# A recurrent layer's convolution and gate product: work moved from GpSimd and VectorE to ScalarE and VectorE, in a decoder step

## The chip, the cores and the metric

One core of a Trainium2 chip runs the whole program. The metric is the device time of one execution in microseconds; three executions of the kernel before were timed. A profile of one execution (not one of the timed ones) gives the start and the length of each instruction on five engines: TensorE (PE, with its weight loads as PEld), VectorE (DVE), ScalarE (ACT), GpSimd (POOL) and SyncE (SP), and of each DMA.

## What is computed

One inference step of two layers over 1032 columns: 1024 positions of one new sequence (the prompt) and one new token for each of 8 samples. Layer 0 mixes with a recurrent block, layer 1 with sliding-window attention; behind each stands a squared-ReLU MLP. The change lies in the recurrent block:

```python
def recurrent_block(x, h0, conv_prev, ...):
    gate, xr = jnp.split(x @ w_in, 2, axis=-1)
    xc, conv_new = causal_conv(xr, conv_prev, conv_w, conv_b)    # 4 taps; conv_new: last 3 rows of xr
    y, h_new = rg_lru(xc, h0, w_a, b_a, w_x, b_x, lam)
    return (y * jax.nn.gelu(gate)) @ w_out, h_new, conv_new

# rg_lru, elementwise but for the two block products and the scan
r = sigmoid(x @ w_a + b_a);  i = sigmoid(x @ w_x + b_x)          # 4 blocks of 256 channels
log_a = -8 * r * softplus(-lam);  a = exp(log_a)
u = sqrt(-expm1(2 * log_a)) * (i * x)
h_t = a_t * h_(t-1) + u_t
```

The prompt starts with zero state. Each sample starts with three old rows of the convolution (`conv_prev`) and its own h. The last three rows of the convolution's input and the last h are outputs, for the prompt and for each sample.

## The kernel before

All activations lie transposed: a tile holds 128 channels (partitions) by 1032 columns, eight tiles (m = 0 to 7) for the 1024 channels. The prompt stands in columns 0 to 1023, the samples in the last 8. Matmuls are made in three passes of fp32r halves: each operand is split into a high part (a cast, on ScalarE) and a low part (a subtraction, on VectorE). A projection works on three chunks of 344 columns, one PSUM bank each, out of a ring of six banks P P P S S T; so a projection takes P P P or S S T, and the next but one needs the banks emptied.

The recurrent layer is a list of stages, `LRU` (L55): `c1 c0 x4 g0 c2 c3 r0 c4 x5 g1 c5 r1 x7 x6 g2 r2 c7 o5 c6 o0 o1 o3 g3 r3 o6 o2 o4 o7`, behind a first stage that makes x0 to x3 together (L1146).

- **x** (`xr_stage`, `conv_evac`, L1122 to L1144): the projection of tile m, 72 matmuls. VectorE empties each bank with a product by the token's norm factor into `xr` (L1127, at high priority). GpSimd then makes the first tap of the convolution and its bias, chunk by chunk, into `xc` (L1128).
- **c** (`conv`, L1130): the three other taps on VectorE over the prompt's columns (L1133); the samples' and the prompt's last rows copied aside for output (L1134, L1135); the samples' three old taps, three VectorE operations on 8 columns (L1137); then the split of `xc` (cast L253 on ScalarE, low part L254 on VectorE).
- **g** (`gates`, L1152): for block kb, r and i of its two tiles: four projections of 18 matmuls from the split tiles 2kb and 2kb+1, each emptied by three sigmoids on ScalarE (L1161, at high priority).
- **r** (`recur`, L1164): for the block's two tiles, x is put together again from its halves by GpSimd (L1170) into the tile `ys[m]`; GpSimd makes i*x (L1171). ScalarE then writes Tanh into `ys[m]` (L1173), Exp over r (L1175), and squares (L1180), each followed by an update of `ys[m]` on VectorE (L1181); then the root (L1183). VectorE makes the product with i*x (L1186), the scan over the prompt (L1187), the samples' single step (L1188, L1189) and a copy of the last h (L1190).
- **o** (`gate_out`, L1194): the gate's projection, GeLU on ScalarE, product into `ys[m]` on VectorE (L1201), split for the output projection.

[...]

Weights arrive on SP's queue two tiles ahead, in two buffers, and are split by `split_unit` (cast L165 on ScalarE, low part L166 on VectorE; two of all units on GpSimd). The states leave by three DMAs on SP's queue behind r3 (L1211 to L1213).

A scheduler sets the order of each engine's instructions when the program is built, from its own estimates; operations marked high priority are put first where they can be. On the chip each engine takes its instructions in that fixed order and waits at each for semaphores of the others. Tiles come from pools (33 buffers of the kind `A`, 12 of `W`); a tile's first writer waits until the buffer's last user is done.

Of the kernel before, what the change touches and what calls it, by code (L numbers as in the profile page):

```python
# [10 lines left out]
F32 = mybir.dt.float32  # L11
F32R = mybir.dt.float32r
AF = mybir.ActivationFunctionType
ALU = mybir.AluOpType
PSUM = bass.MemoryType.PSUM

P = 128
D = 1024
M8 = D // P
SEQ = 1024  # L20
NS = 8
T = SEQ + NS
# [37 lines left out]
def trunk(ctx: ExitStack, tc: tile.TileContext, I, O):  # L60
    nc = tc.nc
    pe, act, dve, pool, sp = nc.tensor, nc.scalar, nc.vector, nc.gpsimd, nc.sync

    cp = ctx.enter_context(tc.tile_pool(name="cp", bufs=1))
# [24 lines left out]
    def nm(s):  # L89
        cnt[0] += 1  # L90
        return f"{s}{cnt[0]}"

    def A(s="a"):
        return ap.tile([P, T], F32, tag="A", name=nm(s))
# [4 lines left out]
    def S(s="s"):  # L99
        return small["pool"].tile([P, CH], F32, tag="S", name=nm(s))  # L100
# [24 lines left out]
    def cs(c):  # L125
        return slice(c * CH, (c + 1) * CH)
# [12 lines left out]
    def V(n, m=0):  # L139
        o, _ = VEC[n]  # L140
        return vec[:, o + m:o + m + 1]

    def VV(n):
        o, w = VEC[n]
        return vec[:, o:o + w]
# [30 lines left out]
    for o in [("x", m) for m in range(4)] + LRU:  # L176
        if o[0] == "g":
            units.append(("gate", o[1], I["w_gate"][o[1]], W))
        elif o[0] in "xo":
            m = o[1] + (8 if o[0] == "x" else 0)  # L180
# [71 lines left out]
    def split_act_dve(hi, lo, src, sl, eng=dve):  # L252
        act.copy(r_(hi[:, sl]), src)  # L253
        eng.tensor_tensor(r_(lo[:, sl]), src, hi[:, sl], ALU.subtract)  # L254
# [831 lines left out]
            ensure(3)  # L1086

    sp.dma_start(con, I["con"])
    cst = cp.tile([P, M8, 4, NS], F32, name="cst")
    sp.dma_start(cst[:, :, 0:3, :], I["conv_state"])  # L1090
    h0 = cp.tile([P, M8, NS], F32, name="h0")
    sp.dma_start(h0, I["h_state"])
    cvp = cp.tile([P, M8, 3], F32, name="cvp")
    hno = cp.tile([P, M8, 1 + NS], F32, name="hno")


    sp8 = cp.tile([P, M8], F32, name="sp8")
    nsp8 = cp.tile([P, M8], F32, name="nsp8")
# [19 lines left out]
    ys = {}  # L1118
# [3 lines left out]
    def conv_evac(m, c, o):  # L1122
        if c == 0:
            xrc[m] = (A("xr"), A("xc"))
        xr, xc = xrc[m]
        with tc.high_priority():
            dve.tensor_tensor(xr[:, cs(c)], o, rx[:, cs(c)], ALU.mult)  # L1127
        pool.tensor_scalar(xc[:, cs(c)], xr[:, cs(c)], V("cw3", m), V("cb", m), ALU.mult, ALU.add)  # L1128

    def conv(m):  # L1130
        xr, xc = xrc.pop(m)
        for d, w in ((1, "cw2"), (2, "cw1"), (3, "cw0")):
            dve.scalar_tensor_tensor(xc[:, d:SEQ], xr[:, 0:SEQ - d], V(w, m), xc[:, d:SEQ], ALU.mult, ALU.add)  # L1133
        dve.tensor_copy(cst[:, m, 3, :], xr[:, SEQ:T])  # L1134
        dve.tensor_copy(cvp[:, m, :], xr[:, SEQ - 3:SEQ])  # L1135
        for k, w in ((2, "cw2"), (1, "cw1"), (0, "cw0")):
            dve.scalar_tensor_tensor(xc[:, SEQ:T], cst[:, m, k, :], V(w, m), xc[:, SEQ:T], ALU.mult, ALU.add)  # L1137
        hi, lo = A("xch"), A("xcl")
        split_act_dve(hi, lo, xc, slice(0, T))
        xcs[m] = (hi, lo)  # L1140

    def xr_stage(m):
        for c, o in enumerate(proj(unit("in", 8 + m, 3), hs)):
            conv_evac(m, c, o)  # L1144

    def xr_first():  # L1146
        ws = [unit("in", 8 + m, 3 - m) for m in range(4)]
        proj_many(ws, hs, conv_evac)
# [15 lines left out]
    def recur(kb):  # L1164
        ms = (2 * kb, 2 * kb + 1)
        for m in ms:
            i = rr[m, 1]
            xh, xl = xcs.pop(m)
            ys[m] = (W if m in (2, 3, 5, 7) else A)("t")
            pool.tensor_tensor(ys[m], xh, xl, ALU.add)  # L1170
            pool.tensor_tensor(i, i, ys[m], ALU.mult)  # L1171
        for m in ms:
            act.activation(ys[m], rr[m, 0], AF.Tanh, scale=sp8[:, m:m + 1])  # L1173
        for m in ms:
            act.activation(rr[m, 0], rr[m, 0], AF.Exp, scale=nsp8[:, m:m + 1])  # L1175
        for m in ms:
            r, t = rr[m, 0], ys[m]
            for c in range(NCH):
                a2 = S("a2")
                act.activation(a2, r[:, cs(c)], AF.Square)  # L1180
                dve.scalar_tensor_tensor(t[:, cs(c)], a2, 1.0, t[:, cs(c)], ALU.add, ALU.mult)  # L1181
        for m in ms:
            act.activation(ys[m], ys[m], AF.Sqrt)  # L1183
        for m in ms:
            r, i, t = rr.pop((m, 0)), rr.pop((m, 1)), ys[m]
            dve.tensor_tensor(i, t, i, ALU.mult)  # L1186
            dve.tensor_tensor_scan(t[:, :SEQ], r[:, :SEQ], i[:, :SEQ], 0.0, ALU.mult, ALU.add)  # L1187
            dve.tensor_tensor(t[:, SEQ:T], r[:, SEQ:T], h0[:, m, :], ALU.mult)  # L1188
            dve.tensor_tensor(t[:, SEQ:T], t[:, SEQ:T], i[:, SEQ:T], ALU.add)  # L1189
            dve.tensor_copy(hno[:, m, :], t[:, SEQ - 1:T])  # L1190

    gos = {}

    def gate_out(m):  # L1194
# [9 lines left out]
        gos[m] = (hi, lo)  # L1204

    stages = {"x": xr_stage, "c": conv, "g": gates, "r": recur, "o": gate_out}
    xr_first()
    for what, i in LRU:
        stages[what](i)
        if (what, i) == ("r", 3):  # L1210
            sp.dma_start(O["conv"][:, :, 3:27].rearrange("p m (k n) -> p m k n", k=3), cst[:, :, 1:4, :])  # L1211
            sp.dma_start(O["conv"][:, :, 0:3], cvp)
            sp.dma_start(O["h"], hno)  # L1213
    gl = [gos[m] for m in range(M8)]
    pin_tables()
    spill, spill0, spill1 = [tc.dram_tile([M8, P, T], F32, name=f"spill{i}") for i in range(3)]
# [130 lines left out]
def _build(arrays):  # L1347
    import concourse.bacc as bacc

    nc = bacc.Bacc("TRN2", target_bir_lowering=False, num_devices=1)  # L1350
    I = {n: nc.dram_tensor(n, a.shape, mybir.dt.from_np(a.dtype), kind="ExternalInput").ap() for n, a in arrays.items()}
    O = {n: nc.dram_tensor("o_" + n, s, F32, kind="ExternalOutput").ap() for n, s in _OUT_SHAPES.items()}
    with tile.TileContext(nc) as tc:
        trunk(tc, I, O)
    return nc
# [23 lines left out]
```

## Time and profile before

| | |
|---|---|
| Timed executions, median of 3 | 2039.52 us (2037.89 to 2041.62) |
| Profiled execution, span from first to last instruction | 2037.0 us |
| First matmul of the first MLP (L529), behind the recurrent layer and its output projection | 348.58 us from the span's start |

No time of the profiled execution outside its span is recorded; its span lies 2.5 us below the timed median. A row of a timeline gives start, length, engine, line, operation and tiles, and in square brackets the idle time of the engine before it with what ended that idle time. A row of groups gives the number of instructions, their sum and mean (ns), and the idle time before them. A row of windows gives the stretch, busy time (and instructions) of PE, PEld, DVE, ACT and POOL, the clock granted to TensorE as a share of full speed, the DMA engines' busy share and GB/s. A row of waits gives who waited for whom, the sum, the number of times and the longest. Matmuls overlap: one of 344 columns is shown with 0.32 us, while the next starts some 0.16 after it.

### The profile page before, as it was taken

Reading aid. Unit: us, or ns where it says so; the run is one execution under the profiler, and the core shown is the slowest. Engines: PE = TensorE matmul, PEld = TensorE weight load, DVE = VectorE, ACT = ScalarE, POOL = GpSimd, SP = SyncE. Lnnn points to the kernel's source line nnn. Section 1 sums busy time; section 2 is a strip of 40 time slices with the busy share of each in tenths; the row PEclk is TensorE's granted clock in tenths of the full one; section 3 lists DMA queues with packets and bytes.
Section 4 is the critical chain, followed back from the end, with each engine's and each line's share of the span. In section 5 each row is a group of like instructions: output and inputs, shape, how many; then the busy total and the mean of one; then the engine's idle time right before and its main releaser. Section 6 shows DMA issues by size and latency. Waiting matters only on the chain.

```text
span 2037.0 us, 38615 instructions
## 1 busy us (share of the span) xinstructions
PE 2002.6 (98%) x15094; PEld 1957.6 (96%) x15094; DVE 1413.5 (69%) x2673; ACT 1051.6 (52%) x2090; POOL 352.1 (17%) x562
## 2 busy tenths in 40 slices
PE   8989999999999999999999999999999999999999
PEld 8989999999999999999988887999999999999999
DVE  8888547876666767766846777569766666777663
ACT  6475635544344645555457776555434435555450
POOL 2541100000001233221003434100000003323220
PEclk9989999999999999999999999999999999999999
DMA  5112142343436778867443435612443447887683
GB/s 175 52 32 55 53 167 84 106 161 135 156 131 207 232 207 218 235 163 184 128 109 84 106 98 180 230 62 82 173 156 131 162 167 235 216 225 220 164 201 105
DMA packets 121047, 304.87 MB, mean 150 GB/s; under 512 B 20888, under 2 KB 53152, under 8 KB 120864
## 3 DMA queue, kind: packets, MB, share of 16 engines
q1 hardware_dynamic: 64864, 135.41, 21.2%
q0 software_dynamic: 28352, 98.30, 18.9%
q10 hardware_dynamic: 27648, 68.70, 9.3%
q8 instruction: 118, 1.93, 0.4%
q14 instruction: 65, 0.53, 0.1%
HBM read 176.22 MB, written 113.44 MB: 142 GB/s over the span
## 4 chain that ended last, share of the span: by engine, by line
PE 74%; issue 10%; DMA 4%; POOL 3%; DVE 3%; ACT 2%; SPq 0%; POOLq 0%; ACTq 0%
PE bD L529 45%; PE bP L226 11%; PE bS L226 6%; PE bP L768 4%; PE bT L226 3%; DMA tl<-hsum 2%; PE bO L889 2%; PE bS L848 1%; PE bT L868 1%; POOL tl L542 1%; DMA spill<-ho 1%; POOL spill L652 1%; PE bN L714 1%; DMA spill<-he 1%; PE bS L796 1%
## 5 line engine op out<-in xcount | busy, mean ns | idle before, releaser
L529 PE MATMUL bD<-op,op 128*128 128x258 f32 x5376 | 648.5, 283 | 0.0
L529 PEld LDWEIGHTS bD<-op,op 128*128 128x128 f32 x5376 | 647.9, 189 | 0.3
L529 PE MATMUL bD<-tl,op 128*128 128x258 f32 x4704 | 571.6, 284 | 4.5 <-ACT ho L633 4.5
L529 PEld LDWEIGHTS bD<-tl,op 128*128 128x128 f32 x4704 | 570.0, 190 | 6.0 <-ACT ho L633 4.9
L542 POOL DMA_DIRECT2D tl<-hsum x196 | 115.1, 672 | 898.3 <-ACT op L395 422.0
L396 DVE TENSOR_TENSOR op<-ws,op 128x512 fp32r<-128x512 f32 (+2 forms) x288 | 168.5, 598 | 84.7 <-ACT op L395 84.6
L633 ACT COPY ho<-bD 128x516 f32<-128x516 f32 x144 | 85.0, 590 | 226.9 <-PE bD L529 226.9
L402 DVE TENSOR_TENSOR tl<-tl 128x516 fp32r<-128x516 f32 x196 | 130.6, 692 | 94.5 <-ACT tl L401 89.3
L395 ACT CAST op<-ws 128x512 fp32r<-128x512 f32 (+2 forms) x288 | 153.4, 550 | 41.4 <-DVE op L396 23.4
L633 ACT COPY he<-bD 128x516 f32<-128x516 f32 x144 | 83.9, 583 | 169.5 <-PE bD L529 169.5
L396 DVE TENSOR_TENSOR op<-raw,op 128x512 fp32r<-128x512 f32 (+2 forms) x216 | 124.0, 597 | 63.0 <-ACT op L395 63.0
L395 ACT CAST op<-raw 128x512 fp32r<-128x512 f32 (+2 forms) x216 | 114.1, 549 | 44.1 <-PE bD L529 20.3
L401 ACT CAST tl<-tl 128x516 fp32r<-128x516 f32 x196 | 115.3, 628 | 3.5 <-DMA tl<-hsum 3.5
L646 ACT ACTIVATE ho<-ho 128x1032 f32<-128x1032 f32 x32 | 34.2, 1069 | 107.3 <-DVE ho L645 107.3
L166 DVE TENSOR_TENSOR wl<-raw,wh 128x1024 fp32r<-128x1024 f32 (+1 forms) x57 | 68.1, 1201 | 25.0 <-ACT wh L165 20.1
L641 DVE TENSOR_TENSOR ho<-bD,ho 128x516 f32<-128x516 f32 x72 | 50.0, 694 | 43.5 <-PE bD L529 43.4
L859 POOL TENSOR_SCALAR se<-se,den 128x256 f32<-128x256 f32 (+1 forms) x128 | 66.0, 520 | 75.9 <-DVE den L857 73.9
L165 ACT CAST wh<-raw 128x1024 fp32r<-128x1024 f32 (+1 forms) x60 | 58.6, 988 | 35.3 <-DMA raw<-w_in 14.7
L652 POOL DMA_DIRECT2D spill<-ho x32 | 28.6, 894 | 259.8 <-DVE ho L641 249.1
L852 DVE CUSTOM_DVE_ANT_0 se<-bS,bias,nsink 128x256 f32<-128x256 f32 (+1 forms) x128 | 56.4, 461 | 21.7 <-PE bS L848 16.6
L855 ACT ACTIVATE se<-se,den 128x257 f32<-128x257 f32 (+1 forms) x128 | 63.0, 495 | 14.7 <-DVE den L852 13.1
L637 DVE TENSOR_TENSOR ho<-bD,ho 128x516 f32<-128x516 f32 x72 | 49.8, 691 | 20.5 <-PE bD L529 13.5
(299 smaller groups left out, 3741.9 us busy)
## 6 DMA issues: line engine op xcount, KB each, us to landing
tl<-hsum POOLq DMA_DIRECT2D x196, 258.0 KB, 7.1
raw<-w_up SPq DMA_DIRECT2D x64, 512.0 KB, 3.8
raw<-w_dn SPq DMA_DIRECT2D x64, 384.0 KB, 6.6
spill<-ho POOLq DMA_DIRECT2D x32, 516.0 KB, 5.7
spill<-he POOLq DMA_DIRECT2D x32, 516.0 KB, 7.1
hsum<-ho ACTq DMA_DIRECT2D x28, 516.0 KB, 3.6
hsum<-he ACTq DMA_DIRECT2D x28, 516.0 KB, 2.7
hsum<-ts ACTq DMA_DIRECT2D x28, 516.0 KB, 3.5
```

Of the source, the lines that this page charges most:

```text
L166: eng.tensor_tensor(r_(lo[:, sl]), raw[:, sl], hi[:, sl], ALU.subtract)
L226: pe.matmul(o, lhsT=r_(wt[:, col(k):col(k) + P]), rhs=r_(xt[:, cs(c)]), start=(k == first and a == 0), stop=(k == final and a == 2))
L395: act.copy(r_(t[:, 0:n]), src)
L396: dve.tensor_tensor(r_(t[:, n:2 * n]), src, t[:, 0:n], ALU.subtract)
L401: act.copy(r_(hi), lo)
L402: dve.tensor_tensor(r_(lo), lo, hi, ALU.subtract)
L529: pe.matmul(d[:, 512 * b:512 * b + QT], lhsT=r_(wt[:, j * P:j * P + P]), rhs=r_(xt[:, QT * b:QT * b + QT]), start=first and j == 0 and a = ...
L542: pool.dma_start(t[:, n:2 * n], src)
L633: last["copy"] = act.copy(t, f).ins
L768: pe.matmul(ps[c], lhsT=r_(wt[:, k * P:k * P + P]), rhs=r_(xt[:, cs(c)]), start=(k == 0 and a == 0), stop=(k == M8 - 1 and a == 2))
L855: act.activation(se[:, u, 256 - n:257], se[:, u, 256 - n:257], AF.Exp, scale=-1.0, bias=dn[:, u:u + 1], accum_out=dn[:, 2 + u:3 + u])
L859: pool.tensor_scalar(e, e, dn[:, 2 + u:3 + u], 0.0, ALU.mult, ALU.add)
```

## The change

Five edits in the recurrent layer:

1. The first tap with its bias leaves `conv_evac` and becomes, in `conv`, one ScalarE activation over all 1032 columns (scale and bias per partition).
2. The three old taps of all samples and tiles are summed once ahead of the layer, by five GpSimd operations, into `scs`; in `conv` one GpSimd addition on 8 columns takes their place.
3. x and i*x move from GpSimd to VectorE. For blocks 0 to 2, x gets a tile of its own, `x2`; block 3 keeps using `ys[m]`.
4. The samples' single step of h moves from VectorE to GpSimd.
5. The copies of states into collecting tiles and SP's three DMAs go. GpSimd's queue issues one DMA of the samples' old rows, one of 11 columns for each tile's last rows (from `xr`), and one of 9 columns for each tile's h (from `ys[m]`).

The host's code that puts the outputs together is fitted to the new layout.

```diff
@@ -1086,13 +1086,18 @@
             ensure(3)
 
     sp.dma_start(con, I["con"])
-    cst = cp.tile([P, M8, 4, NS], F32, name="cst")
-    sp.dma_start(cst[:, :, 0:3, :], I["conv_state"])
+    cst = cp.tile([P, M8, 3, NS], F32, name="cst")
+    sp.dma_start(cst, I["conv_state"])
     h0 = cp.tile([P, M8, NS], F32, name="h0")
     sp.dma_start(h0, I["h_state"])
-    cvp = cp.tile([P, M8, 3], F32, name="cvp")
-    hno = cp.tile([P, M8, 1 + NS], F32, name="hno")
-
+    pool.dma_start(O["conv"][:, :, 0:2 * NS].rearrange("p m (k n) -> p m k n", k=2), cst[:, :, 1:3, :])
+    scs = cp.tile([P, M8, NS], F32, name="scs")
+    scp = cp.tile([P, M8, NS], F32, name="scp")
+    for k in range(3):
+        w = VV(f"cw{k}").unsqueeze(2).broadcast_to([P, M8, NS])
+        pool.tensor_tensor(scp if k else scs, cst[:, :, k, :], w, ALU.mult)
+        if k:
+            pool.tensor_tensor(scs, scs, scp, ALU.add)
 
     sp8 = cp.tile([P, M8], F32, name="sp8")
     nsp8 = cp.tile([P, M8], F32, name="nsp8")
@@ -1125,16 +1130,14 @@
         xr, xc = xrc[m]
         with tc.high_priority():
             dve.tensor_tensor(xr[:, cs(c)], o, rx[:, cs(c)], ALU.mult)
-        pool.tensor_scalar(xc[:, cs(c)], xr[:, cs(c)], V("cw3", m), V("cb", m), ALU.mult, ALU.add)
 
     def conv(m):
         xr, xc = xrc.pop(m)
+        act.activation(xc, xr, AF.Identity, scale=V("cw3", m), bias=V("cb", m))
+        pool.dma_start(O["conv"][:, m, 2 * NS:], xr[:, SEQ - 3:T])
         for d, w in ((1, "cw2"), (2, "cw1"), (3, "cw0")):
             dve.scalar_tensor_tensor(xc[:, d:SEQ], xr[:, 0:SEQ - d], V(w, m), xc[:, d:SEQ], ALU.mult, ALU.add)
-        dve.tensor_copy(cst[:, m, 3, :], xr[:, SEQ:T])
-        dve.tensor_copy(cvp[:, m, :], xr[:, SEQ - 3:SEQ])
-        for k, w in ((2, "cw2"), (1, "cw1"), (0, "cw0")):
-            dve.scalar_tensor_tensor(xc[:, SEQ:T], cst[:, m, k, :], V(w, m), xc[:, SEQ:T], ALU.mult, ALU.add)
+        pool.tensor_tensor(xc[:, SEQ:T], xc[:, SEQ:T], scs[:, m, :], ALU.add)
         hi, lo = A("xch"), A("xcl")
         split_act_dve(hi, lo, xc, slice(0, T))
         xcs[m] = (hi, lo)
@@ -1166,9 +1169,12 @@
         for m in ms:
             i = rr[m, 1]
             xh, xl = xcs.pop(m)
+            x = A("x2") if kb < 3 else None
             ys[m] = (W if m in (2, 3, 5, 7) else A)("t")
-            pool.tensor_tensor(ys[m], xh, xl, ALU.add)
-            pool.tensor_tensor(i, i, ys[m], ALU.mult)
+            if x is None:
+                x = ys[m]
+            dve.tensor_tensor(x, xh, xl, ALU.add)
+            dve.tensor_tensor(i, i, x, ALU.mult)
         for m in ms:
             act.activation(ys[m], rr[m, 0], AF.Tanh, scale=sp8[:, m:m + 1])
         for m in ms:
@@ -1185,9 +1191,9 @@
             r, i, t = rr.pop((m, 0)), rr.pop((m, 1)), ys[m]
             dve.tensor_tensor(i, t, i, ALU.mult)
             dve.tensor_tensor_scan(t[:, :SEQ], r[:, :SEQ], i[:, :SEQ], 0.0, ALU.mult, ALU.add)
-            dve.tensor_tensor(t[:, SEQ:T], r[:, SEQ:T], h0[:, m, :], ALU.mult)
-            dve.tensor_tensor(t[:, SEQ:T], t[:, SEQ:T], i[:, SEQ:T], ALU.add)
-            dve.tensor_copy(hno[:, m, :], t[:, SEQ - 1:T])
+            pool.tensor_tensor(t[:, SEQ:T], r[:, SEQ:T], h0[:, m, :], ALU.mult)
+            pool.tensor_tensor(t[:, SEQ:T], t[:, SEQ:T], i[:, SEQ:T], ALU.add)
+            pool.dma_start(O["h"][:, m, :], t[:, SEQ - 1:T])
 
     gos = {}
 
@@ -1207,10 +1213,6 @@
     xr_first()
     for what, i in LRU:
         stages[what](i)
-        if (what, i) == ("r", 3):
-            sp.dma_start(O["conv"][:, :, 3:27].rearrange("p m (k n) -> p m k n", k=3), cst[:, :, 1:4, :])
-            sp.dma_start(O["conv"][:, :, 0:3], cvp)
-            sp.dma_start(O["h"], hno)
     gl = [gos[m] for m in range(M8)]
     pin_tables()
     spill, spill0, spill1 = [tc.dram_tile([M8, P, T], F32, name=f"spill{i}") for i in range(3)]
@@ -1369,8 +1371,8 @@
     hp = h[0].reshape(1, 1, D)
     hsm = h[1:].reshape(1, NS, D)
     cv = o["conv"].transpose(2, 1, 0).reshape(27, D)
-    cvp = cv[:3].reshape(1, 1, 3, D)
-    cvs = cv[3:].reshape(3, NS, D).transpose(1, 0, 2).reshape(1, NS, 3, D)
+    cvp = cv[2 * NS:2 * NS + 3].reshape(1, 1, 3, D)
+    cvs = np.concatenate([cv[:2 * NS], cv[2 * NS + 3:]]).reshape(3, NS, D).transpose(1, 0, 2).reshape(1, NS, 3, D)
     kp = o["k"].reshape(256, P).T.reshape(1, 1, P, 4, 64)
     vp = o["v"].reshape(1, 1, P, 4, 64)
     ks = o["ks"].reshape(2, P, NS, P).transpose(2, 3, 0, 1).reshape(1, NS, P, 4, 64)
```

In the built programs the matmuls are the same on TensorE, with a few of block 1's fourth projection and x7 in another order. On ScalarE, block 0's twelve sigmoids stand ahead of the first taps of c2 and c3. On VectorE, x5's evacuations stood ahead of r0's updates of `ys`; they now stand behind r0's scans and c4's taps and low part. From the output projection on, the order is the same on every engine.

## Prediction

> **What bounds the kernel now.** The page comes first: one engine is busy nearly all the time.
>
> ```profile
> span 2037.0 us, 38615 instructions
> ## 1 busy us (share of the span) xinstructions
> PE 2002.6 (98%) x15094; PEld 1957.6 (96%) x15094; DVE 1413.5 (69%) x2673; ACT 1051.6 (52%) x2090; POOL 352.1 (17%) x562
> ```
>
> TensorE is the bound, so the change is worth only the time in which it makes TensorE stop more or less. The built programs hold the same matmuls, and behind the recurrent layer all engines' instructions stand in the same order; the answer lies between 40 and 300 us. Next come the list of TensorE's waits there and its timeline.
>
> ```profile
> PE bP L226 <- ACT ri L1161: 6.1, 3, 5.0
> PE bS L226 <- DVE xr L1127: 3.9, 1, 3.9
> ...
> 94.70 0.63 PE L226 MATMUL bP<-xch,wh 128*128 128x344 f32 x3
> ...
> 97.52 0.48 PE L226 MATMUL bS<-xch,wh 128*128 128x344 f32 x2
> ...
> 105.50 1.53 PE L226 MATMUL bP<-xch,wh 128*128 128x344 f32 x3 [4.99 <-ACT ri L1161]
> ...
> 113.82 0.42 PE L226 MATMUL bP<-hh,wh 128*128 128x344 f32 x1 [0.57 <-ACT ri L1161]
> ...
> 139.74 0.32 PE L226 MATMUL bP<-xch,wl 128*128 128x344 f32 x1
> 143.94 1.08 PE L226 MATMUL bS<-xch,wh 128*128 128x344 f32 x2 [3.88 <-DVE xr L1127]
> ...
> 148.59 0.63 PE L226 MATMUL bP<-xch,wh 128*128 128x344 f32 x3
> ...
> 105.50:110.60 5.10, 5.10 (x18) 4.64 (x18) 5.10 (x10) 5.04 (x7) 0.00 (x0) 0.57 0.00 0
> ```
>
> The gates of block 1 are four projections of 18 matmuls. The first runs from 94.70 to 97.52, so 18 take 2.82 at full clock. The second would end at 100.34; the third starts at 105.50, 5.16 late: it waits for banks that ScalarE's sigmoids have not emptied. The last row (busy times, then granted clock) shows what a stop leaves behind: 18 matmuls in 5.10 at a clock of 0.57, 2.28 lost. At 113.82 another 0.57 goes. After 139.74 (+0.16 for the matmul) TensorE stands until 143.94, 4.04, for x6's evacuation on VectorE; the next 18 matmuls last to 148.59, 4.65 instead of 2.82, 1.83 lost. So **13.9** us of stops (5.16+2.28+0.57+4.04+1.83) can be removed; the floor is 13.9 below now.
>
> Why ScalarE was late is in its own timeline:
>
> ```profile
> 83.25 1.43 ACT L1161 ACTIVATE ri<-bP,vec 128x344 f32<-128x344 f32 x3 [1.41 <-PE bP L226]
> 84.55 2.97 ACT L253 CAST xch<-xc 128x1032 fp32r<-128x1032 f32 x3
> 94.25 1.16 ACT L1173 ACTIVATE t<-ri,sp 128x1032 f32<-128x1032 f32 x1 [6.73 <-POOL ri L1171]
> ...
> 97.81 1.28 ACT L1175 ACT_TABLE_LOAD   x1
> 99.11 2.21 ACT L1175 ACTIVATE ri<-ri,nsp 128x1032 f32<-128x1032 f32 x2
> 101.22 2.37 ACT L1180 ACTIVATE a<-ri 128x344 f32<-128x344 f32 x6
> ...
> 104.90 1.42 ACT L1161 ACTIVATE ri<-bP,vec 128x344 f32<-128x344 f32 x3
> ...
> 107.63 1.06 ACT L1183 ACTIVATE t<-t 128x1032 f32<-128x1032 f32 x1
> ```
>
> After block 0's sigmoids ScalarE waits 6.73 for GpSimd's i*x, because Tanh overwrites the tile that holds x; then Exp and squares stand ahead of block 1's first sigmoid (104.90). That wait goes with the change. What comes late next is a matter of the order in which the new program's instructions stand, and there the forecast turns.
>
> **The change, part by part.** GpSimd loses these groups; VectorE loses the small ones below them.
>
> ```profile
> L1128 POOL TENSOR_SCALAR xc<-xr,vec 128x344 f32<-128x344 f32 x24 | 27.0, 1131 | 43.7 <-DVE xr L1127 33.7 <-DVE sp L1113 4.5 <-DVE sp L1110 3.6
> L1171 POOL TENSOR_TENSOR ri<-ri,t 128x1032 f32<-128x1032 f32 x8 | 23.3, 2928 | 12.0 <-ACT ri L1161 11.8
> L1170 POOL TENSOR_TENSOR t<-xch,xcl 128x1032 f32<-128x1032 f32 x8 | 21.1, 2646 | 58.1 <-PE bT L226 40.9 <-issue 10.3 <-ACT ri L1161 4.4
> ...
> L1137 DVE SCALAR_TENSOR_TENSOR xc<-cst,vec,xc 128x8 f32<-128x8 f32 x24 | 9.6, 408 | 0.1
> ...
> L1188 DVE TENSOR_TENSOR t<-ri,h 128x8 f32<-128x8 f32 x8 | 5.5, 690 | 0.0
> ...
> L1173 ACT ACTIVATE t<-ri,sp 128x1032 f32<-128x1032 f32 x8 | 9.2, 1158 | 15.1 <-POOL ri L1171 15.1
> ...
> 54.38 0.51 DVE L1127 TENSOR_TENSOR xr<-bS,rt 128x344 f32<-128x344 f32 x1
> ...
> 63.44 1.22 DVE L254 TENSOR_TENSOR xcl<-xc,xch 128x1032 fp32r<-128x1032 f32 x1
> ...
> 68.47 1.27 DVE L1133 SCALAR_TENSOR_TENSOR xc<-xr,vec,xc 128x1022 f32<-128x1022 f32 x1
> ...
> 110.33 2.28 DVE L1187 TENSOR_TENSOR_SCAN t<-ri,ri 128x1024 f32<-128x1024 f32 x1
> 112.53 0.14 DVE L1188 TENSOR_TENSOR t<-ri,h 128x8 f32<-128x8 f32 x1
> ...
> 143.38 0.93 DVE L1127 TENSOR_TENSOR xr<-bS,rt 128x344 f32<-128x344 f32 x2
> ...
> 73.99 0.99 ACT L1161 ACTIVATE ri<-bS,vec 128x344 f32<-128x344 f32 x2 [4.57 <-PE bS L226]
> ```
>
> GpSimd gives up 71.4 us, none of it on the path beyond the stops above. VectorE gives up 15.1 in the two groups shown and smaller copies, and gains 16 products of the size of L254's, 16*1.22 = 19.5: about even in busy time, but they now stand ahead of r0's scans. ScalarE gains eight activations over 1032 elements with a scale and a bias per partition; the trace has none, so the bounds are the cast of the same length (2.97 for three, 0.99) and Tanh with such a scale (1.158). I take 1.16; over the three on the path below the two ends differ by 0.5.
>
> The order decides. In the new program ScalarE runs **all twelve sigmoids of block 0 before the first taps of c2 and c3**; before, GpSimd had made those early, and VectorE did the other taps meanwhile. VectorE, whose next row is c2's second tap, stands idle until then. And x5's evacuation, which was ahead of r0's updates on VectorE, now stands **behind r0's scans, c4's three taps and c4's lo part**; block 1's second projection writes the banks that it empties. Until block 0's last sigmoid I expect the times of before. c1's last evacuation (54.38) ends at 54.9; from there VectorE's new order has three weight splits of L254's kind, two evacuations, c1's three taps and lo part, c0's three taps, a cast of 1.0 between, and c0's lo part: 3*1.22+0.9+2*(3.81+1.22)+1.0 = 15.6, done at 70.5. Block 0 started some 2.7 of matmuls ahead of its first sigmoid (73.99), at 71.3: covered by 0.8, and each us that this cover lacks would add one. From ScalarE free at 84.55, with the rows above:
>
> 1. c2: activation 1.16, three taps 3*1.27, cast 1.06: 90.6.
> 2. c3, whose activation stands behind that cast: 1.16+3.81+1.06, lo part 1.22: 97.8. (TensorE needs c3 after c2's nine matmuls, at 94.70+1.41 = 96.1; a first stop, swallowed by the next.)
> 3. Tanh, which still waits here, for a buffer that VectorE frees: 2*1.16, table 1.28, Exp 2.21, squares 2.37: 106.0. Beside it VectorE makes x and i*x, 4*1.22 = 4.9, until 102.7: hidden, with 3 to spare.
> 4. Table 1.28 (VectorE's last update fits beside it), first root 1.06: 108.4.
> 5. On VectorE two products and two scans, 2*1.22+2*2.28: 115.4.
> 6. c4: 3*1.27, cast 1.06, lo 1.22: 121.5.
> 7. x5's first evacuation, half of 0.93: **122.0**.
>
> Hand-overs between engines are left out, and so is the overlap of neighbours on one engine; each is under 0.1 per step and they have opposite signs. TensorE thus starts at 122.0 what it started at 97.52: **24.5** late. It comes back from a stop longer than the 5.16 that cost 2.28, so another **2.3**.
>
> The skill's page "TensorE: Matmul & The Clock Gate" (The HAM clock gate) puts the half clock after an idle window at about 3.4 us. By it, as an estimate, the restart would cost 1.7 and the sum would be 0.6 lower; the row of 105.50 has 0.57 over 5.1 us, so it agrees in kind and I keep the row. That page is of the Trainium skill; nothing else here rests on it.
>
> After 122.0 ScalarE has Tanh, two tables and one Exp between the first and the second projection's sigmoids, 1.16+2*1.28+1.1 = 4.8; TensorE has the rest of the second and the third to run meanwhile (2*2.82 and the slow start). x6's evacuation behind r1's scans comes out within 0.5 us of TensorE's need, with a GpSimd weight split beside the VectorE split ahead of it:
>
> ```profile
> 136.94 3.02 POOL L166 TENSOR_TENSOR wl<-raw,wh 128x1024 fp32r<-128x1024 f32 x1 [8.80 <-PE bS L226]
> 137.68 2.30 DVE L1188 TENSOR_TENSOR t<-ri,h 128x8 f32<-128x8 f32 x1
> ```
>
> An operation on 8 elements took 2.30 while GpSimd's split ran, against 0.14 at 112.53. So up to 3 at that place; I take **1.5**. The 13.9 go, since each stop has lost its cause or lies under the new one.
>
> The state edits I cost at nothing. The taps of the samples' old rows are five GpSimd instructions on 64 elements, and the first transfer leaves once the state is there:
>
> ```profile
> L1090 SPq DMA_DIRECT2D cst<-conv_state x1: 652/652/652, 19.0 to 19.0; - x1
> DMA to landing us min/median/max: 6.4/6.4/6.4
> L542 POOL DMA_DIRECT2D tl<-hsum x196 | 115.1, 672 | 898.3 <-ACT op L395 422.0
> tl<-hsum POOLq DMA_DIRECT2D x196, 258.0 KB, 7.1
> ```
>
> The state lands at 25.4; c1 needs the sum only behind its last evacuation, at 54.9. The transfer of 1024 short rows, if each cost what one of 128 rows costs at 672 ns, would hold GpSimd 5.4: covered 5 times. Sixteen small transfers hold it 0.7 each, in places where it is otherwise idle. SP loses three issues that nobody waited for.
>
> Sum: 24.5+2.3+1.5-13.9 = **+14.4**. Against the profiled execution that is 2037.0+14.4 = 2051.4 of span; on the median, 2.5 above that span, 2053.9. I forecast **2054**.
>
> **Rivals.** (a) *Faster.* VectorE, free of GpSimd's long operations (the rows at 136.94 and 137.68, and 408 ns mean for L1137's eight elements), runs ahead of TensorE, and x5's evacuation is not held up. It decides from the point where that evacuation is done by 97.5; then all stops go: 2039.5-13.9 = 2025.6. For it: 71.4 us of GpSimd work vanish. Against it: my chain already uses undisturbed durations, and it ends 24.5 later. The Trainium skill's page "SBUF — State Buffer" (Who interferes with whom) says the same of VectorE with two SBUF inputs against GpSimd, and the row at 137.68 agrees.
>
> (b) *No change.* If c2's and c3's activations slipped in under block 0's sigmoids, steps 1 and 2 (13.3) would be over by 84.55: 14.4-13.3 = +1.1, 2040.6. Against it: each engine takes its instructions in order.
>
> (c) *Slower still.* The new tiles of h leave by transfers from GpSimd's queue, and VectorE's product with the gate overwrites that tile, so it waits for the landing, with the evacuations of o5 and o6 behind it. Two issues of 0.7 and 7.1 to the landing, 8.5, lie under one 72-matmul projection (4*2.82 = 11.3). If landing took twice as long, 15.6-11.3 = 4.3 would show, twice: 2054+8.6, about 2063. "SBUF — State Buffer" (the "DVE blocks DMA" trap) of the Trainium skill says that VectorE can keep GpSimd from writing a transfer's descriptors; no row here shows that, and an estimate of one scan's wait at both places would give 4.6.
>
> (d) *The change does not do what it says* is half true and in my sum: Tanh has a tile of its own, yet waits.
>
> **How the numbers follow.** Forecast 75%, (a) 9%, (b) 5%, (c) 11%. The chain has some 25 instructions; 8 us off it would be a third, which I take as its bound below; (c) is the bound above. Range 2046 to 2062: it leaves out (a), (b) and the upper half of (c), about 20%. A measurement of this kernel tells 0.2%, 4 us, from no change. Faster 0.09, same 0.05, slower 0.86.
>
> **What would show it.** In the new profile: one stop of TensorE of over 20 us near 99 to 122, released by VectorE's evacuation of x5; a granted clock near 0.6 for 5 us after it; VectorE idle from about 76 to 86, released by ScalarE's activation of c2; no wait of Tanh for i*x. I am wrong if TensorE's longest stop is under 10 us, if x5's evacuation is done before 115, or if the loss lies behind 300 us.

## The result, and the profile after

The changed kernel takes 2052.09 us (median of 5, 2049.82 to 2055.02), the kernel before, timed beside it, 2039.36 (median of 5, 2037.89 to 2041.62). The ratio is 1.0062, 95% interval 1.0051 to 1.0073: **12.7 us slower**. The profiled execution's span is 2050.3, 13.3 above that of before.

First the page of the changed kernel, its span and busy times.

```profile
span 2050.3 us, 38606 instructions
## 1 busy us (share of the span) xinstructions
PE 2003.2 (98%) x15094; PEld 1958.1 (96%) x15094; DVE 1404.0 (68%) x2625; ACT 1060.9 (52%) x2097; POOL 324.2 (16%) x568
```

TensorE's busy time is 0.6 above that of before, so nearly all of the 13.3 is time in which it stands. GpSimd lost 27.9 and VectorE 9.5 of busy time, ScalarE gained 9.3: the sums alone would not tell which way the time goes. TensorE's waits between 40 and 340 us (who waited for whom, the sum, how often, the longest) do:

```profile
PE bS L226 <- DVE xr L1132: 22.7, 1, 22.7
PE bP L226 <- ACT xch L253: 1.0, 1, 1.0
PE bP L226 <- ACT ri L1164: 0.7, 1, 0.7
PE bP L226 <- DVE xcl L254: 0.5, 1, 0.5
```

Before, these waits were 10.6 in all, the longest 5.0; now they are 25.1 (the four shown and one of 0.2), and **one stop of 22.7** makes up nine tenths. The long stops of before are gone. TensorE's timeline gives its place:

```profile
95.70 0.74 PE L226 MATMUL bP<-xch,wh 128*128 128x344 f32 x3 [0.95 <-ACT xch L253]
...
96.97 0.74 PE L226 MATMUL bP<-xcl,wh 128*128 128x344 f32 x3 [0.53 <-DVE xcl L254]
...
120.91 1.08 PE L226 MATMUL bS<-xch,wh 128*128 128x344 f32 x2 [22.72 <-DVE xr L1132]
...
126.29 0.64 PE L226 MATMUL bP<-xch,wh 128*128 128x344 f32 x3
```

The first two are the small waits for c3's halves. At 120.91 starts block 1's second projection, which before started at 97.52; it writes the banks that VectorE empties of x5. Its 18 matmuls last until 126.29. The windows give the clock granted during the stop and behind it (stretch, its length, busy time of PE, PEld, DVE, ACT and POOL, then the clock):

```profile
95.00:130.00 35.00, 11.05 (x51) 10.28 (x51) 21.47 (x22) 23.33 (x29) 9.37 (x8) 0.66 0.00 1
...
120.91:126.90 5.99, 5.99 (x22) 5.85 (x23) 0.80 (x2) 5.90 (x8) 0.54 (x1) 0.56 0.01 1
126.90:132.00 5.10, 5.10 (x34) 4.93 (x33) 0.00 (x0) 3.52 (x8) 0.00 (x0) 1.00 0.02 3
```

TensorE is busy for 11.05 of these 35 us, and for the first 6 us behind the stop its clock is 0.56; from 126.9 it is full again. What TensorE waited for is read from the two engines that hand work to each other meanwhile. ScalarE's timeline:

```profile
83.02 1.25 ACT L1136 ACTIVATE xc<-xr,vec 128x1032 f32<-128x1032 f32 x1
88.31 1.06 ACT L253 CAST xch<-xc 128x1032 fp32r<-128x1032 f32 x1 [4.03 <-issue]
...
94.60 1.05 ACT L253 CAST xch<-xc 128x1032 fp32r<-128x1032 f32 x1 [4.08 <-DVE xc L1139]
96.95 2.30 ACT L1179 ACTIVATE t<-ri,sp 128x1032 f32<-128x1032 f32 x2 [1.30 <-DVE xcl L254]
...
102.67 2.37 ACT L1186 ACTIVATE a<-ri 128x344 f32<-128x344 f32 x6
...
118.12 1.05 ACT L253 CAST xch<-xc 128x1032 fp32r<-128x1032 f32 x1 [8.61 <-DVE xc L1139]
```

And VectorE's:

```profile
84.31 3.92 DVE L1139 SCALAR_TENSOR_TENSOR xc<-xr,vec,xc 128x1023 f32<-128x1023 f32 x3 [11.44 <-ACT xc L1136]
...
95.68 1.24 DVE L254 TENSOR_TENSOR xcl<-xc,xch 128x1032 fp32r<-128x1032 f32 x1 [1.17 <-ACT xch L253]
...
99.12 2.37 DVE L1177 TENSOR_TENSOR ri<-ri,x 128x1032 f32<-128x1032 f32 x2
...
109.75 4.47 DVE L1193 TENSOR_TENSOR_SCAN t<-ri,ri 128x1024 f32<-128x1024 f32 x2
114.14 3.89 DVE L1139 SCALAR_TENSOR_TENSOR xc<-xr,vec,xc 128x1023 f32<-128x1023 f32 x3
119.20 1.23 DVE L254 TENSOR_TENSOR xcl<-xc,xch 128x1032 fp32r<-128x1032 f32 x1 [1.17 <-ACT xch L253]
120.35 0.93 DVE L1132 TENSOR_TENSOR xr<-bS,rt 128x344 f32<-128x344 f32 x2
```

Read the two together as one chain: c2's first tap on ScalarE (83.02), VectorE's other taps, which had stood idle 11.44 for it (84.31), the cast (88.31), c3 in the same way, then Tanh, Exp, squares and roots on ScalarE, scans on VectorE (109.75), c4's taps (114.14), cast (118.12) and low part, and only then x5's evacuation (120.35). ScalarE also loads a table ahead of Exp and ahead of the roots (99.27 and 105.06, 1.28 each); between the sigmoids and Tanh it loads none. At most places one engine works and the other waits, and TensorE waits for both. Neither engine is full there: of the 35 us VectorE is busy for 21.47 and ScalarE for 23.33.

### The profile page after: what moved, and what is told of

The parts are those of the page before. It is cut to its first block, busy times and chain, and to the rows that moved or that the text cites. A ratio compares the mean times of both kernels' runs of the same rounds, so it can differ in the third digit from the quotient of the medians.

```text
span 2050.3 us, 38606 instructions
## 1 busy us (share of the span) xinstructions
PE 2003.2 (98%) x15094; PEld 1958.1 (96%) x15094; DVE 1404.0 (68%) x2625; ACT 1060.9 (52%) x2097; POOL 324.2 (16%) x568
## 4 chain that ended last, share of the span: by engine, by line
PE 76%; issue 11%; DVE 4%; DMA 4%; ACT 3%; POOL 3%; SPq 0%; POOLq 0%; ACTq 0%; DVEq 0%
PE bD L529 45%; PE bP L226 11%; PE bS L226 6%; PE bP L768 4%; PE bT L226 3%; DMA tl<-hsum 2%; PE bO L889 1%; PE bS L848 1%; PE bT L868 1%; POOL spill L652 1%; POOL tl L542 1%; PE bN L714 1%; DMA spill<-he 1%; DVE xc L1139 1%; DMA spill<-ho 1%
## 5 line engine op out<-in xcount | busy, mean ns | idle before, releaser
L529 PE MATMUL bD<-op,op 128*128 128x258 f32 x5376 | 648.3, 283 | 0.0
L529 PEld LDWEIGHTS bD<-op,op 128*128 128x128 f32 x5376 | 647.8, 190 | 0.3
L529 PE MATMUL bD<-tl,op 128*128 128x258 f32 x4704 | 568.4, 283 | 3.3 <-ACT ho L633 3.3
L529 PEld LDWEIGHTS bD<-tl,op 128*128 128x128 f32 x4704 | 567.0, 190 | 4.6 <-ACT ho L633 3.7
L395 ACT CAST op<-ws 128x512 fp32r<-128x512 f32 (+2 forms) x288 | 153.4, 550 | 42.4 <-DVE op L396 23.4
```

The costliest lines, as they stand in the source:

```text
L395: act.copy(r_(t[:, 0:n]), src)
L529: pe.matmul(d[:, 512 * b:512 * b + QT], lhsT=r_(wt[:, j * P:j * P + P]), rhs=r_(xt[:, QT * b:QT * b + QT]), start=first and j == 0 and a = ...
```

## The experiments

Theories for where the 12.7 come from. **O (order)** is that of the prediction: the first tap on ScalarE stands behind all twelve sigmoids of block 0, VectorE's taps wait for it, and x5's evacuation stands at the end of that chain, behind r0's scans and c4. **V** (VectorE's load): x and i*x, 16 long products on VectorE, make its queue late. **S** (states): the transfers and the small operations on GpSimd hold something up. Each kernel was timed in five rounds beside the kernel before on the same chip; "first L529" is the start of the first matmul of the MLP behind the layer in TensorE's timeline, 348.42 before and 361.46 after.

| kernel | us | ratio to before, 95% | first L529 |
|---|---|---|---|
| all edits (after) | 2052.09 | 1.0062 [1.0051, 1.0073] | 361.46 |
| E1: x and states, without the tap | 2040.53 | 1.0002 [0.9993, 1.0012] | 351.56 |
| E2: the tap alone | 2067.02 | 1.0134 [1.0118, 1.0150] | 375.27 |
| E3: x and i*x alone | 2042.55 | 1.0016 [1.0007, 1.0026] | 351.55 |
| E4: the states alone | 2040.90 | 1.0007 [0.9995, 1.0018] | 351.07 |
| E9: tap and x | 2057.11 | 1.0085 [1.0072, 1.0098] | 365.35 |
| E10: tap and states | 2058.09 | 1.0093 [1.0080, 1.0106] | 369.39 |
| E5: all edits, the tap at high priority | 2043.49 | 1.0024 [1.0015, 1.0033] | 354.72 |
| E6: all edits, x5 ahead of r0 | 2042.74 | 1.0015 [1.0006, 1.0025] | 353.72 |
| E7: x alone, x5 ahead of r0 | 2040.86 | 1.0008 [0.9999, 1.0018] | 348.96 |
| E8: before, x5 ahead of r0 | 2043.89 | 1.0019 [1.0009, 1.0028] | 351.94 |

**E1: all edits but the first tap**, which goes back to GpSimd.

```diff
             dve.tensor_tensor(xr[:, cs(c)], o, rx[:, cs(c)], ALU.mult)
+        pool.tensor_scalar(xc[:, cs(c)], xr[:, cs(c)], V("cw3", m), V("cb", m), ALU.mult, ALU.add)
 ...
-        act.activation(xc, xr, AF.Identity, scale=V("cw3", m), bias=V("cb", m))
```

> The changed kernel with the first tap back on GpSimd, chunk by chunk behind each evacuation; everything else of the change stays. Theory O (the loss is the place of the first taps of c2 and c3 behind block 0's sigmoids in ScalarE's order, and of x5's evacuation behind the chain that this lengthens): VectorE no longer idles from 73 to 84; the two convolutions (13.3 in the chain) are out of it; the stop of 22.7 shrinks to some 9 to 11, still ended by x5's evacuation; time 2035 to 2041, about that of before. Rival V (VectorE is slowed by the products x and i*x that it took over) and rival S (the state steps and transfers on GpSimd's queue): the stop stays above 18 and the time at 2048 or more.

Measured 2040.53, no difference from before. TensorE's timeline of this kernel has the same stop, shorter:

```profile
108.34 1.08 PE L226 MATMUL bS<-xch,wh 128*128 128x344 f32 x2 [9.28 <-DVE xr L1132]
```

The loss hangs on the tap; x on VectorE and the states together cost nothing that can be measured. V and S are out as its causes.

**E2: the first tap alone**, as one activation on ScalarE, in the kernel before.

```diff
-        pool.tensor_scalar(xc[:, cs(c)], xr[:, cs(c)], V("cw3", m), V("cb", m), ALU.mult, ALU.add)
 ...
         xr, xc = xrc.pop(m)
+        act.activation(xc, xr, AF.Identity, scale=V("cw3", m), bias=V("cb", m))
```

> The kernel before with one edit: the first tap as one ScalarE activation in conv. x and i*x stay on GpSimd, the states as before. Theory O: the whole loss is here, and more, since Tanh again waits for i*x: a stop of 21 to 26 before block 1's second projection, time 2051 to 2060. Rivals V and S: nothing of what they blame is in this kernel, so 2036 to 2042.

Measured 2067.02: the direction is O's, the size is not, it is 15 above the whole change. TensorE's timeline:

```profile
126.09 1.07 PE L226 MATMUL bS<-xch,wh 128*128 128x344 f32 x2 [21.46 <-DVE xr L1127]
...
170.10 1.08 PE L226 MATMUL bS<-xch,wh 128*128 128x344 f32 x2 [7.35 <-DVE xr L1127]
```

The big stop ends 5.2 later than in the changed kernel, and a second one of 7.35 stands at x6's evacuation. VectorE's timeline shows what made both:

```profile
90.59 1.28 DVE L1133 SCALAR_TENSOR_TENSOR xc<-xr,vec,xc 128x1023 f32<-128x1023 f32 x1
...
94.09 3.45 DVE L1133 SCALAR_TENSOR_TENSOR xc<-xr,vec,xc 128x1022 f32<-128x1022 f32 x1
...
160.35 2.31 DVE L1188 TENSOR_TENSOR t<-ri,h 128x8 f32<-128x8 f32 x1
...
164.78 2.25 DVE L1189 TENSOR_TENSOR t<-t,ri 128x8 f32<-128x8 f32 x1
...
167.07 2.29 DVE L1190 COPY hno<-t 128x9 f32<-128x9 f32 x1
```

A tap takes 1.28 alone and 3.45 at 94.09; three operations on 8 or 9 elements take 2.25 to 2.31 each, ahead of x6's evacuation. GpSimd's timeline has long operations at those times, x at 90.81, a weight split at 157.25 and x again at 162.60:

```profile
90.81 5.65 POOL L1170 TENSOR_TENSOR t<-xch,xcl 128x1032 f32<-128x1032 f32 x2 [67.49 <-DVE xcl L254]
...
157.25 5.39 POOL L166 TENSOR_TENSOR wl<-raw,wh 128x1024 fp32r<-128x1024 f32 x1 [12.19 <-ACT wh L165]
162.60 6.73 POOL L1170 TENSOR_TENSOR t<-xch,xcl 128x1032 f32<-128x1032 f32 x2
```

The Trainium skill's page "SBUF — State Buffer" (Who interferes with whom) says that a VectorE instruction with two SBUF inputs contends with a GpSimd instruction that reads SBUF. The rows with two inputs agree. The copy at 167.07 has one input and was held as well, which that sentence does not cover. The trace gives the price, up to some 2.2 for a VectorE instruction that is caught. In the whole change the edits of x and of the states take the two kinds off: x's products leave GpSimd, and the samples' steps leave VectorE. E9 and E10 test that.

**E3: x and i*x alone** on VectorE, in their own tile, in the kernel before.

```diff
+            x = A("x2") if kb < 3 else None
 ...
-            pool.tensor_tensor(ys[m], xh, xl, ALU.add)
-            pool.tensor_tensor(i, i, ys[m], ALU.mult)
+            if x is None:
+                x = ys[m]
+            dve.tensor_tensor(x, xh, xl, ALU.add)
+            dve.tensor_tensor(i, i, x, ALU.mult)
```

> The kernel before with one edit: x and i*x on VectorE, x in its own tile for blocks 0 to 2. Theory O: Tanh no longer waits for GpSimd, the 6.73 of ScalarE's wait go; x5's evacuation still stands behind r0's scans, so a stop of 6 to 10 in place of the 5.2, and the second stop (4.0 at 144) goes with GpSimd's long operations: 2032 to 2040. Rival V: slower than before, 2046 or more, with a stop of over 15.

Measured 2042.55, a miss for O and for V: 3 us slower. TensorE's timeline:

```profile
107.15 0.66 PE L226 MATMUL bS<-xch,wh 128*128 128x344 f32 x1 [9.49 <-DVE xr L1127]
...
146.35 0.84 PE L226 MATMUL bS<-xch,wh 128*128 128x344 f32 x2 [2.10 <-DVE xr L1127]
```

Tanh's wait of 6.73 for i*x has gone, and the stop for ScalarE's sigmoids with it. In its place x5's evacuation is late: 9.49, where O had 6 to 10. A second stop of 2.10 stayed, at x6's evacuation: GpSimd's weight split stays where it was, and beside it (139.31, 2.40) one of VectorE's taps takes 3.42.

**E4: the state edits alone** (samples' old taps summed once, their step of h on GpSimd, states leaving by GpSimd's transfers), in the kernel before; the diff is edits 2, 4 and 5 of the change.

> The kernel before with the state edits alone: old taps summed once, the samples' step of h on GpSimd, states out by GpSimd's queue; first tap, x and i*x stay on GpSimd. Theory O: VectorE sheds some 19 of small operations that had waited for GpSimd; between 6 faster than before and no change, 2033 to 2040. Rival S: slower, 2045 or more, with new waits of VectorE or TensorE behind the transfers.

Measured 2040.90, no difference that can be told: S's 2045 or more did not come, and neither did the gain that I had thought possible. The list of waits says why:

```profile
PE bP L226 <- ACT ri L1164: 5.0, 2, 4.4
PE bS L226 <- DVE xr L1132: 2.8, 1, 2.8
PE bS L226 <- DVE g L1202: 2.5, 1, 2.5
```

The first two are 2.2 shorter than before (6.1 and 3.9), but a new stop of 2.5 takes it back. It is at the evacuation behind o5's gate product, that of o0, and VectorE's timeline has a wait ahead of it:

```profile
184.10 0.52 DVE L1204 TENSOR_TENSOR t<-t,g 128x344 f32<-128x344 f32 x1 [3.21 <-DMA o_h<-t]
```

The product overwrites the tile of h and waits 3.21 for the landing of the transfer that reads it. That is the mechanism of S, and of the prediction's rival (c). The wait is longer than the stop, though not the only thing that can make this evacuation late: E8, without these transfers, has a stop of 2.8 there. In the changed kernel VectorE waits for such a landing too, 1.95, and no matmul stops behind it. So S is out as the cause of the 12.7, and not as a mechanism.

**E5: the whole change, the activation at high priority.** The operations are the same; c4's taps move ahead of r0's updates.

```diff
-        act.activation(xc, xr, AF.Identity, scale=V("cw3", m), bias=V("cb", m))
+        with tc.high_priority():
+            act.activation(xc, xr, AF.Identity, scale=V("cw3", m), bias=V("cb", m))
```

> The changed kernel with the first-tap activation marked high priority. Same operations on the same engines; in the built order c2's activation moves up by two sigmoids only, and c4's activation and three taps move ahead of r0's updates, into time in which VectorE waited for ScalarE's squares. Theory O prices this by the chain: step 6 loses its three taps (3.9) and step 1 about 0.9, and c4's cast no longer waits, about 1: the stop of 22.7 shrinks to 16 to 18, time 2045 to 2048. Rival W (the stop is a matter of how much work stands on VectorE and ScalarE, not of where c4 stands): unchanged, 2050 to 2054.

Measured 2043.49. TensorE's timeline:

```profile
115.67 1.08 PE L226 MATMUL bS<-xch,wh 128*128 128x344 f32 x2 [18.78 <-DVE xr L1132]
```

c4's taps (100.12 to 104.03) now lie beside ScalarE's Exp and squares, and the chain ends 5.2 earlier. The stop came out 0.8 longer than expected, the time 1.5 lower than the lower end.

**E6: the whole change, with x5 ahead of r0**, so that the scheduler places x5's evacuation ahead of r0's work. The operations are the same.

```diff
-    "c1 c0 x4 g0 c2 c3 r0 c4 x5 g1 c5 r1 x7 x6 g2 r2 c7 o5 c6 o0 o1 o3 g3 r3 o6 o2 o4 o7").split()]
+    "c1 c0 x4 g0 c2 c3 x5 r0 g1 c4 c5 r1 x7 x6 g2 r2 c7 o5 c6 o0 o1 o3 g3 r3 o6 o2 o4 o7").split()]
```

> The changed kernel with the list of stages in another order: x5 ahead of r0, block 1's gates ahead of c4. The same operations on the same engines. Theory O: x5's evacuation now stands ahead of r0's products on VectorE, so the stop before block 1's second projection falls from 22.7 to under 3; since c4, c5 and x7's evacuation now stand behind r0's scans instead, a stop of 8 to 14 appears later, before block 2; time 2037 to 2044. Rival W: about 2052, since no work went.

Measured 2042.74. TensorE's timeline has no stop of 22 any more, but this one:

```profile
144.26 0.99 PE L226 MATMUL bP<-xch,wh 128*128 128x344 f32 x2 [13.30 <-DVE xr L1132]
```

With the same operations the ratio falls from 1.0062 to 1.0015, 9.6 of the 12.7, when the evacuation stands at another place in VectorE's queue: O is shown by this. What stays has moved to the next evacuation behind r0, c4 and c5, that of x7.

**E7 and E8: can the floor be had?** E7 is E3's edit with E6's order, without the tap; E8 is the kernel before with E6's order, its control.

> The kernel before with x and i*x on VectorE in a tile of their own, and x5 ahead of r0, block 1's gates ahead of c4 in the list of stages. First tap on GpSimd, states as before. Theory O: Tanh waits for nothing, x5's evacuation stands ahead of r0's products, so no stop of TensorE over 4; 4 to 10 faster than before, 2029 to 2036. Rival V (VectorE's products cost what they take): 2040 or more.

> The kernel before with the new list of stages alone (x5 ahead of r0, block 1's gates ahead of c4), the control for the run before it. x and i*x stay on GpSimd and Tanh waits for them. Theory O: a stop of 4 to 8 by ScalarE stays, since r0's chain still starts when GpSimd is done: 2037 to 2044. If the order of stages alone were the gain, 2029 to 2036.

E7 measured 2040.86, where O had hoped for 2029 to 2036; E8 measured 2043.89, as expected, with a stop of 7.8 by ScalarE's sigmoids. E7's waits:

```profile
PE bP L226 <- ACT ri L1161: 6.2, 4, 3.4
PE bP L226 <- DVE g L1202: 3.8, 1, 3.8
PE bS L226 <- ACT ri L1161: 1.0, 1, 1.0
```

No stop is above 4, as expected; but there are six in this list, 11.0 together, against four of 10.0 from ScalarE's `ri` and VectorE before. Sigmoids (the longest stop, 3.4, ends behind a sigmoid at 146.84, which stands behind two roots of block 1) and o5's evacuation now come late. The stops that the prediction counts as removable (13.9 with their slow starts) are not bound to one wait; in E3, E4, E7 and E8 what went came back at the next hand-over.

**E9 and E10: which edit gives back what the tap costs?**

> The kernel before with two of the edits: the first tap as one ScalarE activation, and x with i*x on VectorE in their own tile; the state edits are left as before. The tap alone gave 2067, the whole change 2052, so the other edits give back some 15 beside the tap. Theory O: it is the x edit that gives them back. With the tap alone GpSimd makes x and i*x for block 0 between 90.8 and 110.4, on the chain: ScalarE's Tanh waits 3.47 and 2.14 for it, and beside it three of VectorE's taps take 3.4 instead of 1.27, 6.4 together. O expects here one TensorE stop of 21 to 25 us released by VectorE's evacuation of x5 and a time of 2049 to 2055. Rival (the state edits give it back, by taking 24 small operations off VectorE): a stop like that of the tap alone with a second one of 5 or more behind it, and 2060 to 2067.

> The kernel before with two of the edits: the first tap as one ScalarE activation, and the state edits (samples' old taps summed once, their step of h on GpSimd, states leaving by GpSimd's transfers); x and i*x stay on GpSimd. Theory O (the x edit gives back what the tap alone costs above the whole change): VectorE's taps still take over 3 us beside GpSimd's x, Tanh still waits for GpSimd's i*x, and the time is 2060 to 2067. Rival (the state edits give it back): 2049 to 2055, with no tap of VectorE above 2 us between 80 and 115.

Measured 2057.11 and 2058.09. Each lies between the two expectations, 2 us outside O's and 3 outside the rival's: both edits give back, the x edit 10 of E2's 27 us and the state edits 8 (0.0049 and 0.0041 of 2039, from the ratios). That it is the x edit alone falls. E9's TensorE timeline:

```profile
121.77 1.08 PE L226 MATMUL bS<-xch,wh 128*128 128x344 f32 x2 [23.46 <-DVE xr L1127]
...
160.51 1.08 PE L226 MATMUL bS<-xch,wh 128*128 128x344 f32 x2 [2.18 <-DVE xr L1127]
```

The first stop ends 0.9 later than in the changed kernel (VectorE's small operations stand in the chain again), and the second stop is there. In E9's VectorE timeline, ahead of x6's evacuation, stands the one small operation that is caught beside GpSimd's weight split (155.03, 3.76):

```profile
156.53 2.29 DVE L1192 TENSOR_TENSOR t<-t,ri 128x8 f32<-128x8 f32 x1
```

In E10 the x edit is missing, so GpSimd's x still lies beside VectorE's taps and Tanh waits for it again (3.54 and 2.14 in its ScalarE timeline); its second stop is down from 7.35 to 2.34:

```profile
164.40 0.84 PE L226 MATMUL bS<-xch,wh 128*128 128x344 f32 x2 [2.34 <-DVE xr L1132]
```

With these the eight combinations of tap, x and states are all measured. The tap costs in each pair: 0.0134 alone, 0.0069 beside x, 0.0086 beside the states, 0.0060 beside both (differences of the ratios in the table), 27, 14, 18 and 12 us. Without the tap, no combination is more than 0.0016 from before.

None of the kernels was faster than the one before. An order of stages that lets both the evacuations and the sigmoids stand early was not found; whether there is one stays open.

## Why the prediction was right, point by point

The forecast was 2054, the range 2046 to 2062; measured 2052.09. The steps of the chain, by the rows above:

| step | forecast ends | measured | row it is read from |
|---|---|---|---|
| ScalarE free of block 0's sigmoids | 84.55 | 83.02 | start of the first activation |
| 1. c2's cast | 90.6 | 89.4 | 88.31 + 1.06 |
| 2. c3's low part | 97.8 | 96.9 | 95.68 + 1.24 |
| 3. squares | 106.0 | 105.0 | 102.67 + 2.37 |
| 5. scans | 115.4 | 114.2 | 109.75 + 4.47 |
| 6. c4's low part | 121.5 | 120.4 | 119.20 + 1.23 |
| 7. TensorE starts | 122.0 | 120.91 | its own row |

- **Length of the chain:** 37.45 forecast, 37.89 measured. The activation with scale and bias takes 1.25, outside both of my bounds (the cast's 0.99 and Tanh's 1.16, which I took). The prediction speaks of three on the path, but its steps hold two (c2's and c3's; c4's was done in time); they make 0.2 of the 0.4.
- **Its start:** "until block 0's last sigmoid I expect the times of before" failed by 1.5. TensorE reached block 0's gates 0.8 earlier (its waits ahead of 45 us are 4.8 in all, before 5.7), so the first sigmoid started at 73.20 instead of 73.99. The other 0.7 was lost before between the first and the second projection of the block: three weight loads of TensorE, from 74.22 on, wait 0.24 each for VectorE's evacuation of x4, which starts at 73.67. In the changed kernel it starts at 70.38, and none waits. So the term of 24.5 came out as 120.91-97.52 = 23.4.
- **Slow clock:** 18 matmuls took 126.29-120.91 = 5.38 instead of 2.82, 2.6 lost; forecast 2.3. The Trainium skill's page "TensorE: Matmul & The Clock Gate" (The HAM clock gate) would have given 1.7 by the estimate in the prediction; the measurement decides for the longer one: 0.56 over 6 us.
- **x6's evacuation, +1.5:** came out at some 0.5. No matmul waits there, but two of TensorE's weight loads do, 0.21 and 0.24. The price was nearer for another kernel: E9, the change without the state edits, has a stop of 2.18 there. The row of 2.30 that I took it from is a small operation on VectorE that the change itself moves to GpSimd. In the changed kernel x6's evacuation stands at 156.79 and GpSimd's split starts at 158.61, behind it:

```profile
158.61 4.08 POOL L166 TENSOR_TENSOR wl<-raw,wh 128x1024 fp32r<-128x1024 f32 x1
```

- **Stops removed, -13.9:** right as a count; between 126.29 and 361.46 only a stop of 0.7 is left, and one of 0.6 stood there before. I read it as the long stop's doing, in which every other queue catches up: without the tap, E1 has waits of 11.9 again between 40 and 340 us (10.6 before). That was argued, not tried by itself.
- **Sum:** 23.4+2.6-13.9 = 12.1, against 13.0 measured at the first L529 (361.46-348.42; the 348.58 ahead of the prediction is from the chain that ended last, where the matmul ahead of it ends then). The missing 0.9 is in weight loads, which the list of TensorE's waits doesn't count: the two at x6's evacuation, and two that wait 0.41 and 0.24 for o5's gate product, 1.1 in all. The first of each pair:

```profile
157.77 0.19 PEld L226 LDWEIGHTS bS<-xch,wh 128*128 128x128 f32 x1 [0.21 <-DVE xr L1132]
...
189.57 0.19 PEld L226 LDWEIGHTS bP<-hh,wh 128*128 128x128 f32 x1 [0.41 <-DVE g L1205]
```

  The mechanism came out as forecast, and the terms missed by -1.1, +0.3, -1.0 and, at o5, +0.7. That these partly cancel is luck.
- **States at nothing:** right for the edits alone (E4). Beside the tap they are worth some 5 to 8 us: E9 less the whole change, 0.0023 of 2039, and E2 less E10, 0.0041. This was missed, and would have counted had the state edits not been there. The first transfer, of 1024 short rows, held GpSimd 1.06 (its row at 25.20), where I allowed 5.4.
- **Tanh:** waits 1.30 for VectorE's low part (ScalarE's row at 96.95), not for i*x, which VectorE has done by 101.5, ahead of the first updates. That half of the edit does what it says.
- **Rivals:** (a) fell: x5's evacuation was at 120.35, not by 97.5. (b) fell: VectorE's first tap of c2 came at 84.31, behind the sigmoids. (c) fell: no matmul of TensorE behind 126 us waits for a gate product, and the weight loads at o5 wait ahead of any landing. The wait on VectorE that (c) speaks of is there, but TensorE doesn't stop behind it; h's transfers land 1.7 to 3.7 after their issue, where (c) took 7.1:

```profile
193.45 0.52 DVE L1207 TENSOR_TENSOR t<-t,g 128x344 f32<-128x344 f32 x1 [1.95 <-DMA o_h<-t]
```

## What to carry to other kernels

A step that moves from an idle engine to a busy in-order one brings with it the place in that engine's queue: ask what stands ahead of it there, and which buffer is freed by what now stands behind it. Here 1.25 us of work per tile went to an engine that is half idle, and the pair of engines that hand work to each other became one chain of 38 us ahead of a PSUM evacuation. When a stop is to be removed, look for the next hand-over that is nearly late; if there is one, the gain ends there.

## What the runs showed of the hardware that was not expected

GpSimd's operations on 8 elements take 0.20 at the least and up to 3.27 beside VectorE's operations with two inputs. GpSimd's timeline of the changed kernel:

```profile
90.59 0.20 POOL L1140 TENSOR_TENSOR xc<-xc,scs 128x8 f32<-128x8 f32 x1 [4.94 <-ACT xc L1136]
...
182.08 3.27 POOL L1194 TENSOR_TENSOR t<-ri,h 128x8 f32<-128x8 f32 x1 [7.68 <-DVE ri L1192]
```

3.27 is longer than any one of VectorE's instructions there (a product 1.22, a scan 2.28), so it can be held by more than one of them. TensorE waited for none of this; VectorE's gate product at 193.45 waited for a transfer that stands behind these steps in GpSimd's queue. The other way round, a VectorE instruction caught beside GpSimd's long ones loses up to some 2.2 us, whether it has 8 elements (2.29 against 0.14) or 1022 (3.45 against 1.28).
